# Memory tokens and first weights from one DMA queue, and query norms by four transposes, in a projection kernel with side work

## The chip, the cores and the metric

The kernel runs on one core of a Trainium2 chip. The metric is device time in microseconds (us) of one execution; lower is better. A core has a matrix engine (TensorE, PE in the profile, with its weight loads apart as PEld), VectorE (DVE), ScalarE (ACT), GpSimd (POOL), and SyncE (SP), which here only issues transfers. ACT issues a few transfers too. PSUM has eight banks of 128 x 512 f32, into which PE writes.

## The reference

One layer of a hybrid decoder over 256 tokens of width 2048. A combined input projection feeds a gated DeltaNet (12 query/key heads, 24 value heads of 128) and a four-head cross-attention into 256 memory tokens; both results are multiplied by a SiLU gate and go through an output projection. Cut to what the change touches:

```python
mem_n = rms_norm(mem, mem_norm_g)                       # 256 memory tokens
kv = jnp.einsum("bmd,de->bme", mem_n, w_kv)             # V and K of the memory
...
q = jnp.repeat(l2_norm(q), rep, axis=2) * DN_HEAD_DIM ** -0.5
k = jnp.repeat(l2_norm(k), rep, axis=2)
...
o = gated_delta_rule(q, k, v, g, beta)
o = rms_norm(o, out_g)
```

`l2_norm` of a query divides by the root of its sum of squares. The kernel leaves q unnormalised and puts that sum, `eq`, into the epsilon of the output's RMS norm, where it has the same effect.

## The kernel before

**Projections.** All big products are streams of weight tiles. `PLAN` lists 273 weight loads of 128 x 1024 f32 (512 KB): first the memory's V and K (`V0`, `V1`, `K0`, `K1`), then `ab`, and x, k, z, v, q column tiles, at the end the output projection (`o0` to `o3`). `wraw` issues a load into a tile `st` (five buffers); `wnext` splits it into a rounded half `hi` (ACT, a CAST, L342) and the rest `lo` (DVE, a subtraction, L346), both in one tile `wt` (four buffers). A projection in the form `proj_b` multiplies each tile by three products per half (activation hi by weight hi, hi by lo, lo by hi) and two row blocks, twelve matmuls of 128 x 512 into two banks (`pb`); `proj_a` does eight pairs of a 512- and a 256-wide matmul into one bank (`pa`).

**Start.** V0 and V1 go in turn over the same memory tokens. `memT` arrives as eight tiles `mst` of two 128-row steps each; `mem_prep` scales a step by a gain out of `prm` and splits it (`mkt`). The first step's `mkt` is made by a DVE TENSOR_SCALAR and a DVE SCALAR_TENSOR_TENSOR; the others' first half by ACT. `mem_prep` also squares the tokens (`msq`); `mem_stats` adds the squares, sums them over partitions on PE (`pss`), raises them to the power -1/2 on POOL (`msm`), and then `vm_done` scales V out of its bank (`vmh` on ACT, `vml` on DVE), which frees the bank. V0 and K0 use the two banks of pool `A`, V1 and K1 those of pool `pa`. Nine matmuls on zeros (`warm`) run on PE ahead of all.

**Order of the side work.** What is not a projection (convolutions, decays, triangular inverses `pm`, the delta rule, norms) is written as Python generators. While the program is written out, a clock `now` estimates PE's time; a generator that wants PE yields `("pe", gather)` and is entered into the stream when its `gather` time has passed, with all others that wait at that moment (`step_side`). `GATHER` (delta rule) is 0.5 us, `GATHER_Y` (the transposes `pyT` of finished outputs, generator `split_y`) 4.0 us. So these numbers set where in PE's program order such work stands; the engines run their queues in order. Up to `PINNED` = 45 us the order is kept as written.

**Delta rule.** `delta(g)` handles two pairs of heads, six groups in all: `pkq`, `pU`, `pO`, and at its end the second chunk's `pO` with the query norms. The query norms before: ACT squares q of each pair (tile `q2`, shown as `q`, read from `kq`), PE multiplies the squares by a column of ones (`pqs`, four one-column matmuls, f32, two records each) into a bank of pool `m`, and DVE reads four columns out of it (`eq`). Pool `m` has two banks and also serves `pkq`, `pyT`, `pm` and others.

**Names in the profile.** Nearly all operations go through two helpers, so their line is L86 (PE and SP) or L103 (ACT, DVE, POOL); the tile names tell them apart.

Of the kernel before, what the change touches and what calls it, by code (L numbers as in the profile page):

```python
# [21 lines left out]
NB = 2  # L22
C = 128
# [9 lines left out]

LOOK = 2
WARM = 9
GATHER = 0.5
GATHER_Y = 4.0
XPACE = 3.0
HOP = 0.25
PINNED = 45.0  # L40
# [32 lines left out]
def hybrid_kernel(ctx: ExitStack, tc: tile.TileContext, x, xT, memT, W, prm_d, cst_d, out):  # L73
# [3 lines left out]
    def pin(ins):  # L77

        return tc.keep_in_program_order(ins) if PINNED is None or now[0] < PINNED else ins
# [65 lines left out]
    def S2(name, shape, dt=F32):  # L145
        return s2p.tile([128] + list(shape), dt, name=name, tag="s2")
# [17 lines left out]
    def PS(tag, name):  # L164
        idle[tag].remove(min(idle[tag]))
        pt = ps.tile([128, 512], F32, name=name, tag=tag, bufs=PB[tag])
        held[id(pt)] = (tag, pt)
        return pt
# [4 lines left out]
    def give(pt, t):  # L173

        idle[held.pop(id(pt))[0]].append(t)
# [54 lines left out]
    def until(cond):  # L230
        while not cond():
            yield POLL
# [45 lines left out]
    def wraw():  # L278
# [20 lines left out]
        dma[0] = max(dma[0], free.pop(0)) + 1.46  # L299
        if n < 2:  # L300

            w = [slice(a * 512, (a + 1) * 512) for a in range(2)]
            if n == 0:
                pin(nc.scalar.dma_start(dst[:, w[0]], data[:, w[0]]))
                pin(nc.scalar.dma_start(prm[:, 0:P_CW], prm_d[:, 0:P_CW]))
            else:
                sy.dma_start(dst[:, w[0]], data[:, w[0]])
            sy.dma_start(dst[:, w[1]], data[:, w[1]])
            first_loads(1) if n == 0 else mem_load(2)
        else:  # L310
            sy.dma_start(dst, data)
            if 2 * n < NKT:
                mem_load(2 * n)
        wpos[0] += 1
        raws.append((n, kind, st, src, dma[0] + 2.0))

    def first_loads(a):

        if a == 0:
            mst[0] = S2("mst", [512])  # L320
        w = slice(a * 256, (a + 1) * 256)
        sy.dma_start(mst[0][:, w], memT[0][:, w])

    def wnext():
        while wpos[0] < len(PLAN) and free:
# [119 lines left out]
    def mem_load(k0):  # L445

        mst[k0 // 2] = S2("mst", [512])
        dma[0] += 0.75
        sy.dma_start(mst[k0 // 2], memT[k0 // 4][:, k0 % 4 * 256 : k0 % 4 * 256 + 512])
# [13 lines left out]
            se.activation(msq[-1], mst[k2], AF.Square)  # L463


    memq = [(2,), (3, 4), (5,), (6, 7), (8,), (9, 10), (11,), (12, 13), (14,), (15,)]

    def mem_piece(s):
        if not ahead:
# [773 lines left out]
    def delta(g):  # L1243
# [77 lines left out]
        for w in range(4):  # L1321
            se.activation(oq[:, w, :], B[:, w * C : (w + 1) * C], AF.Copy, scale=egc[:, 4 * g + w : 4 * g + w + 1])
        give(B, se.end)
        q2 = S2("q2", [2, 256])
        for i, p in enumerate(pp):
            se.activation(q2[:, i, :], KQ[p][:, 1, :], AF.Square)
        yield from pe_soon(GATHER)
        yield from until(lambda: spare("B") and spare("m"))
        B, pq = PS("B", "pO"), PS("m", "pqs")
        for w, i, h in heads:  # L1330
            mm(B[:, w * C : (w + 1) * C], aT[i][:, 1, h, :], u1[:, w, :], start=True, stop=True)
        for b in range(NB):
            for i in range(2):
                mm(pq[:, 2 * b + i : 2 * b + i + 1], q2[:, i, b * C : (b + 1) * C], ones, start=True, stop=True)
        yield 0.2
        ve.tensor_tensor(out=o[1], in0=B.rearrange("c (h e) -> c h e", h=4), in1=oq, op=ALU.add)
        give(B, ve.end)

        eq, e4 = SM("eq", [4], 2), SM("e4", [3, NB, 4], 2)
        ve.tensor_scalar(out=eq, in0=pq[:, 0:4], scalar1=EPS, scalar2=EPS * 128, op0=ALU.add, op1=ALU.mult)  # L1340
        give(pq, ve.end)
        ready.add(f"d{g}")
        yield
        for b in range(NB):
            for w in range(4):
                junk = SM("ojunk", [C])
                se.activation(junk, o[b][:, w, :], AF.Square, accum_out=e4[:, 0, b, w : w + 1])
        yield
        yield from until(lambda: {f"z{g}0", f"z{g}1"} <= ready)
        ev = [e4[:, a].rearrange("c b (i h) -> c (b i) h", h=2) for a in range(2)]  # L1350
        ve.scalar_tensor_tensor(out=ev[1], in0=ev[0], scalar=1.0 / 128,
# [54 lines left out]
            return proj_b(kts, x_act, "A" if t in (0, 6) else "pa", z_done(t))  # L1406
        return proj_a({"k": k_tile_done, "q": q_done}[kind](t))

    first_loads(0)
    spawn(mem_stats(), 8.0)  # L1410
    spawn(tok_prep(), 8.0)
    spawn(blank(), 100.0)
# [95 lines left out]
```

## Time and profile before

| | |
|---|---|
| median of three runs | 856.51 us (855.76 to 857.1) |
| the profiled execution, its own time | 857.04 us |
| its span in the trace | 855.3 us |
| granted clock of TensorE, mean over the span | 1.00 of full speed |
| PE busy | 848.0 us, 99% |
| weight loads of PE busy | 709.7 us, 83% |
| DVE busy | 618.1 us, 72% |
| ACT busy | 538.1 us, 63% |
| POOL busy | 46.5 us, 5% |

The span runs from the first to the last instruction; 1.74 us of the execution lie around it. The profiled execution is 0.53 us above the median of the runs. Busy shares are means over stages; which engine sets the time in a stage is read from the waits and from the chain of work that ended last.

### The profile page before, as it was taken

Reading aid. Unit: us, or ns where it says so; the run is one execution under the profiler, and the core shown is the slowest. Engines: PE = TensorE matmul, PEld = TensorE weight load, DVE = VectorE, ACT = ScalarE, POOL = GpSimd, SP = SyncE. Lnnn points to the kernel's source line nnn. Section 1 sums busy time; section 2 is a strip of 40 time slices with the busy share of each in tenths; the row PEclk is TensorE's granted clock in tenths of the full one; section 3 lists DMA queues with packets and bytes.
Section 4 is the critical chain, followed back from the end, with each engine's and each line's share of the span. In section 5 each row is a group of like instructions: output and inputs, shape, how many; then the busy total and the mean of one; then the engine's idle time right before and its main releaser. Section 6 shows DMA issues by size and latency. Waiting matters only on the chain.

```text
span 855.3 us, 13175 instructions
## 1 busy us (share of the span) xinstructions
PE 848.0 (99%) x4790; PEld 709.7 (83%) x4790; DVE 618.1 (72%) x1080; ACT 538.1 (63%) x929; POOL 46.5 (5%) x45
## 2 busy tenths in 40 slices
PE   9999999999999999999999999999999999999998
PEld 6888888888888888888888888788888888888886
DVE  6878886657779974788889989568886655454442
ACT  7656665798644765995966676679775654333331
POOL 1000000000000000001100202000010000000000
PEclk9999999999999999999999999999999999999999
DMA  9965566448677886869877769686755547666650
GB/s 344 335 218 177 171 189 165 146 147 263 197 208 241 263 243 180 261 210 266 226 243 218 227 214 279 198 242 222 227 158 169 186 142 265 214 210 205 199 197 25
DMA packets 145433, 181.59 MB, mean 212 GB/s; under 512 B 24824, under 2 KB 115824, under 8 KB 145368
## 3 DMA queue, kind: packets, MB, share of 16 engines
q1 hardware_dynamic: 145080, 180.47, 67.0%
q8 instruction: 37, 0.61, 0.3%
q10 hardware_dynamic: 288, 0.28, 0.1%
q14 instruction: 28, 0.23, 0.1%
HBM read 167.58 MB, written 6.89 MB: 204 GB/s over the span
## 4 chain that ended last, share of the span: by engine, by line
PE 95%; ACT 2%; DMA 1%; DVE 1%; issue 1%; SPq 0%; DVEq 0%
PE pb L86 72%; PE pa L86 13%; PE pO L86 2%; PE pU L86 2%; PE pm L86 1%; PE pkq L86 1%; PE pyT L86 1%; ACT dec L103 1%; DVE wt L346 1%; PE pqs L86 1%; PE pkk L86 1%; DMA erow<-dgc 0%; DMA st<-W_d 0%; ACT L103 0%; PE pab L86 0%
## 5 line engine op out<-in xcount | busy, mean ns | idle before, releaser
L346 DVE TENSOR_TENSOR wt<-st,wt 128x1024 fp32r<-128x1024 f32 (+1 forms) x275 | 331.9, 1212 | 164.9 <-ACT wt L342 161.2
L342 ACT CAST wt<-st 128x1024 fp32r<-128x1024 f32 (+1 forms) x275 | 286.3, 1045 | 224.3 <-PE pb L86 180.6
L86 PE MATMUL pb<-wt,hkt 128*128 128x512 f32 x1536 | 361.8, 392 | 0.0
L86 PEld LDWEIGHTS pb<-wt,hkt 128*128 128x128 f32 x1536 | 284.7, 188 | 58.7 <-DVE wt L346 0.4
L86 PE MATMUL pb<-wt,yhi 128*128 128x512 f32 x512 | 158.0, 390 | 0.0
L86 PE MATMUL pa<-hkt,wt 128*128 128x512 f32 (+1 forms) x768 | 142.8, 342 | 0.4 <-DVE wt L346 0.3
L86 PEld LDWEIGHTS pa<-hkt,wt 128*128 128x128 f32 x768 | 117.9, 188 | 18.3 <-DVE wt L346 1.0
L86 PEld LDWEIGHTS pb<-wt,yhi 128*128 128x128 f32 x512 | 95.7, 188 | 19.6
L86 PE MATMUL pb<-wt,ylo 128*128 128x512 f32 x256 | 99.7, 389 | 0.0
L86 PE MATMUL pb<-wt,mkt 128*128 128x512 f32 x384 | 88.6, 391 | 0.9 <-ACT wt L342 0.9
L86 PEld LDWEIGHTS pb<-wt,mkt 128*128 128x128 f32 x384 | 71.6, 188 | 16.8 <-ACT wt L342 1.8
L86 PEld LDWEIGHTS pb<-wt,ylo 128*128 128x128 f32 x256 | 48.1, 188 | 10.1
L103 ACT ACT_TABLE_LOAD x31 | 39.8, 1283 | 1.4 <-DVE acc L103 1.0
L103 DVE SCALAR_TENSOR_TENSOR acc<-raw,prm,acc 128x255 f32<-128x255 f32 (+2 forms) x72 | 34.2, 476 | 3.6 <-ACT acc L103 3.2
L103 DVE TENSOR_TENSOR inT<-inXT,inN 96x1 f32<-96x1 f32 (+22 forms) x92 | 29.1, 342 | 3.2 <-DMA inN<-dN 2.4
L103 DVE TENSOR_REDUCE inXT<-inT 96x1 f32<-96x1 f32 (+22 forms) x92 | 28.6, 337 | 0.7
L103 POOL TENSOR_TENSOR e<-e,mhalf 128x8 f32<-128x8 f32 x6 | 20.8, 3472 | 120.5 <-DVE e L103 120.5
L103 DVE TENSOR_TENSOR vc<-vc 128x512 f32<-128x512 f32 x36 | 24.5, 682 | 0.1
L103 POOL TENSOR_TENSOR srk<-skt,mhalf 128x4 f32<-128x4 f32 x6 | 7.0, 1175 | 224.6 <-DVE skt L103 145.6
L103 DVE SCALAR_TENSOR_TENSOR o<-o,e,zs 128x128 f32<-128x128 f32 x48 | 14.0, 345 | 7.0 <-POOL e L103 7.0
L103 ACT ACTIVATE ojunk<-o 128x128 f32<-128x128 f32 x48 | 14.4, 301 | 7.0 <-DVE o L103 4.9
L103 DVE TENSOR_TENSOR vc<-vc,vw 128x512 f32<-128x512 f32 x24 | 16.4, 683 | 2.8 <-DMA vc<-vs 2.8
(202 smaller groups left out, 693.9 us busy)
## 6 DMA issues: line engine op xcount, KB each, us to landing
st<-W_d SPq DMA_DIRECT2D x271, 512.0 KB
erow<-dgc SPq DMA_DIRECT2D x24, 256.0 KB
vw<-dtap SPq DMA_DIRECT2D x24, 256.0 KB
dN<-dec SPq DMA_DIRECT2D x12, 256.0 KB
n<-dN SPq DMA_DIRECT2D x12, 256.0 KB
vc<-vs SPq DMA_DIRECT2D x12, 224.0 KB
vc<-vc SPq DMA_DIRECT2D x12, 224.0 KB
xraw<-xT_d SPq DMA_DIRECT2D x8, 256.0 KB
```

The lines of the kernel that those rows point to most:

```text
L86: return lambda *a, **k: pin(getattr(self.eng, op)(*a, **k))
L103: return pin(getattr(self.eng, op)(*a, **k))
L342: pin(se.eng.copy(hi[:, w] if parts > 1 else hi, st[:, w] if parts > 1 else src))
L346: pin(ve.eng.tensor_tensor(out=lo[:, w] if parts > 1 else lo, in0=st[:, w] if parts > 1 else src, in1=hi[:, w] if parts > 1 else hi, op=AL ...
```

## The change

It has three parts. **Start:** ACT's queue issues only the gains `prm`; SP issues the first weight halves and the memory tokens in one row, and from there one memory tile after every second weight load. The memory steps are prepared one per load where they were sometimes two and sometimes one. **Gathering:** `GATHER` becomes 0.0 and `GATHER_Y` 0.5. **Query norms:** four PE transposes (`pqT`) put q of the four query blocks into a bank of pool `m`; ACT squares the bank into `q2` (128 x 512), which frees it; DVE sums each 128 columns (TENSOR_REDUCE) and applies the epsilon.

```diff
-GATHER = 0.5
-GATHER_Y = 4.0
+GATHER = 0.0
+GATHER_Y = 0.5
...
         if n < 2:
 
-            w = [slice(a * 512, (a + 1) * 512) for a in range(2)]
             if n == 0:
-                pin(nc.scalar.dma_start(dst[:, w[0]], data[:, w[0]]))
+                mst[0] = S2("mst", [512])
                 pin(nc.scalar.dma_start(prm[:, 0:P_CW], prm_d[:, 0:P_CW]))
-            else:
-                sy.dma_start(dst[:, w[0]], data[:, w[0]])
-            sy.dma_start(dst[:, w[1]], data[:, w[1]])
-            first_loads(1) if n == 0 else mem_load(2)
+            for a in range(2):
+                w, t = slice(a * 512, (a + 1) * 512), slice(a * 256, (a + 1) * 256)
+                sy.dma_start(dst[:, w], data[:, w])
+                if n == 0:
+                    sy.dma_start(mst[0][:, t], memT[0][:, t])
         else:
             sy.dma_start(dst, data)
-            if 2 * n < NKT:
-                mem_load(2 * n)
+
+        if n % 2 and n < 12 or n == 12:
+            mem_load(n + 1 if n % 2 else 14)
...
-    memq = [(2,), (3, 4), (5,), (6, 7), (8,), (9, 10), (11,), (12, 13), (14,), (15,)]
+    memq = [(k,) for k in range(2, 12)] + [(12, 13), (14,), (15,)]
...
-        q2 = S2("q2", [2, 256])
-        for i, p in enumerate(pp):
-            se.activation(q2[:, i, :], KQ[p][:, 1, :], AF.Square)
         yield from pe_soon(GATHER)
         yield from until(lambda: spare("B") and spare("m"))
-        B, pq = PS("B", "pO"), PS("m", "pqs")
+        B, pq = PS("B", "pO"), PS("m", "pqT")
         for w, i, h in heads:
             mm(B[:, w * C : (w + 1) * C], aT[i][:, 1, h, :], u1[:, w, :], start=True, stop=True)
-        for b in range(NB):
-            for i in range(2):
-                mm(pq[:, 2 * b + i : 2 * b + i + 1], q2[:, i, b * C : (b + 1) * C], ones, start=True, stop=True)
+        for w in range(4):
+
+            tr(pq[:, w * C : (w + 1) * C], KQ[pp[w % 2]][:, 1, w // 2 * C : (w // 2 + 1) * C])
...
-        ve.tensor_scalar(out=eq, in0=pq[:, 0:4], scalar1=EPS, scalar2=EPS * 128, op0=ALU.add, op1=ALU.mult)
-        give(pq, ve.end)
+        q2 = S2("q2", [4, C])
+        se.activation(q2.rearrange("c w e -> c (w e)"), pq, AF.Square)
+        give(pq, se.end)
...
+        ve.tensor_reduce(out=eq, in_=q2, axis=AX.X, op=ALU.add)
+        ve.tensor_scalar(out=eq, in0=eq, scalar1=EPS, scalar2=EPS * 128, op0=ALU.add, op1=ALU.mult)
```

The order of instructions moves at three places that matter below. The first is the start of SP's queue. The transfers into `st` are weights, those into `mst` memory tokens; 128x512 is half a weight tile. Before:

```order
L86 DMA mst<-memT_d 128x256
L86 DMA st<-W_d 128x512
L86 DMA mst<-memT_d 128x256
L86 DMA st<-W_d 128x512 x2
L86 DMA mst<-memT_d 128x512
L86 DMA st<-W_d 128x1024
L86 DMA mst<-memT_d 128x512
L86 DMA st<-W_d 128x1024
L86 DMA mst<-memT_d 128x512
```

The same place of the change:

```order
L86 DMA st<-W_d 128x512
L86 DMA mst<-memT_d 128x256
L86 DMA st<-W_d 128x512
L86 DMA mst<-memT_d 128x256
L86 DMA st<-W_d 128x512 x2
L86 DMA mst<-memT_d 128x512
L86 DMA st<-W_d 128x1024 x2
L86 DMA mst<-memT_d 128x512
L86 DMA st<-W_d 128x1024 x2
```

The first weight half, before issued by ACT ahead of `prm`, now stands at the head of SP's queue; up to the third weight tile (the first of 128x1024) the same transfers stand ahead, and behind it one memory tile follows two weight tiles.

The second place is PE's program at the end of V0, whose banks are `pb_116` and `pb_169` before, `pb_114` and `pb_163` in the change; V1's are the other two, and the first of K0 is the bank that comes last. Before:

```order
L86 MATMUL pss<-cst,msq 128x1 x2
L86 MATMUL pb_182<-wt,mkt 128x512 x3
L86 MATMUL pb_206<-wt,mkt 128x512 x3
L86 MATMUL pb_182<-wt,mkt 128x512 x3
L86 MATMUL pb_206<-wt,mkt 128x512 x3
L86 MATMUL pb_116<-wt,mkt 128x512 x3
L86 MATMUL pb_169<-wt,mkt 128x512 x3
L86 MATMUL pb_116<-wt,mkt 128x512 x3
L86 MATMUL pb_169<-wt,mkt 128x512 x3
L86 MATMUL pb_116<-wt,mkt 128x512 x6
L86 MATMUL pb_169<-wt,mkt 128x512 x6
```

The change:

```order
L86 MATMUL pb_114<-wt,mkt 128x512 x6
L86 MATMUL pb_163<-wt,mkt 128x512 x6
L86 MATMUL pss<-cst,msq 128x1 x2
L86 MATMUL pb_176<-wt,mkt 128x512 x3
L86 MATMUL pb_197<-wt,mkt 128x512 x3
L86 MATMUL pb_176<-wt,mkt 128x512 x3
L86 MATMUL pb_197<-wt,mkt 128x512 x3
L86 MATMUL pb_176<-wt,mkt 128x512 x6
L86 MATMUL pb_197<-wt,mkt 128x512 x6
L86 MATMUL pb_561<-wt,mkt 128x512 x6
```

The sum of the memory's squares (`pss`) stood ahead of V1's last but two and V0's last two loads and now stands behind them, 36 matmuls later: behind 168 of V's 192, where it stood behind 132.

The third place is the end of a group of the delta rule, on PE and on ACT. PE at the end of the second group, before:

```order
L86 MATMUL pa<-hkt,wt 128x512
L86 MATMUL pa<-hkt,wt 128x256
L86 MATMUL pO<-u_4711,aT 128x128 x4
L86 MATMUL pqs<-cst,q_4718 128x1 x4
L86 MATMUL pa<-hkt,wt 128x512
```

The change:

```order
L86 MATMUL pa<-hkt,wt 128x512
L86 MATMUL pa<-hkt,wt 128x256
L86 MATMUL pO<-u_4650,aT 128x128 x4
L86 MATMUL pqT<-cst,kq 128x128 x4
L86 MATMUL pa<-hkt,wt 128x512
```

ACT at the end of the first group, the change:

```order
L336 CAST wt<-st 128x1024
L103 ACTIVATE q_4120<-pqT 128x512
L103 ACTIVATE ojunk,e_4119<-o 128x128 x4
L336 CAST wt<-st 128x1024
L103 COPY raw<-pa 128x512
L103 ACTIVATE dec<-erow,gcc 128x128 x2
L103 ACT_TABLE_LOAD
L103 ACTIVATE kq<-acc 128x256
L103 ACTIVATE dec<-erow,gcc 128x128 x2
L103 ACTIVATE acc<-raw,prm 128x256
L103 ACTIVATE vc<-vc 128x512 x2
L103 ACTIVATE vc<-vc,sV 128x128 x8
```

The transposes stand where the one-column matmuls stood (in the first group alone, ahead of `pO`). On ACT the square of the transposed queries stands behind a CAST; a little later a row of side work runs from `raw` to `vc` with no CAST in it.

## Rows read from the trace of the kernel before

**Rows 1.** The page, parts 1 and 4: busy time by engine; the chain by engine.

```profile
PE 848.0 (99%) x4790; PEld 709.7 (83%) x4790; DVE 618.1 (72%) x1080; ACT 538.1 (63%) x929; POOL 46.5 (5%) x45
...
PE 95%; ACT 2%; DMA 1%; DVE 1%; issue 1%; SPq 0%; DVEq 0%
```

**Rows 2.** Waits of PE: us in total, times, longest us.

```profile
PE pb L86 <- ACT wt L342: 0.9, 1, 0.9
PE pa L86 <- DVE wt L346: 0.3, 1, 0.3
```

**Rows 3.** Timeline, first 12 us: start, length, instruction, idle before and its releaser.

```profile
0.72 0.41 ACTq L304 DMA_DIRECT2D st<-W_d  x1
...
0.73 0.39 SPq L86 DMA_DIRECT2D mst<-memT_d  x1
...
1.16 0.46 ACTq L305 DMA_DIRECT2D prm<-prm_d  x1
...
1.21 4.02 PE L86 MATMUL warm<-warm 128*128 128x512 bf16 x9 [1.21 <-DVE warm L103]
...
4.61 1.36 ACT L342 CAST wt<-st 128x512 fp32r<-128x512 f32 x2 [1.67 <-DMA st<-W_d]
...
5.61 0.35 DVE L103 TENSOR_SCALAR mkt<-mst,prm 128x256 fp32r<-128x256 f32 x1 [4.46 <-DMA prm<-prm_d]
...
6.12 4.27 PE L86 MATMUL pb<-wt,mkt 128*128 128x512 f32 x17 [0.89 <-ACT wt L342]
...
8.91 1.05 ACT L342 CAST wt<-st 128x1024 fp32r<-128x1024 f32 x1 [0.73 <-DMA st<-W_d]
...
9.99 1.23 DVE L346 TENSOR_TENSOR wt<-st,wt 128x1024 fp32r<-128x1024 f32 x1 [0.30 <-ACT wt L342]
```

**Rows 4.** Busy time by engine from the first projection matmul to `pss`.

```profile
core 0: us, PE busy (x) PEld busy (x) DVE busy (x) ACT busy (x) POOL busy (x), PEclk, DMA share, GB/s
5.90:36.46 30.56, 30.34 (x135) 24.91 (x135) 28.27 (x44) 25.69 (x42) 0.00 (x0) 1.00 1.01 380
```

**Rows 5.** Chain of work that ended last, up to 40 us: start, length, what.

```profile
6.12 30.34 PE pb L86 x132
```

**Rows 6.** The chain at the end of the first group.

```profile
407.18 0.56 PE pqs L86 x6
407.75 3.31 PE pb L86 x14
```

**Rows 7.** The chain at the end of the second group.

```profile
459.97 1.53 PE pa L86 x9
...
462.39 0.79 PE pqs L86 x8
463.18 2.19 PE pa L86 x12
```

**Rows 8.** The chain around four transposes of the cross-attention's queries.

```profile
196.53 0.44 PE xpT L86 x4
196.97 3.23 PE pb L86 x14
```

**Rows 9.** Tile `pyT`: minimum/median/maximum ns of one, first and last start.

```profile
L86 PE MATMUL pyT<-cst,o x48: 270/272/273, 639.6 to 712.5; 128*128 128x128 f32 x48
```

**Rows 10.** Tiles `dg` and `q`: a DVE sum over 128x512, and ACT's squares.

```profile
L103 DVE TENSOR_REDUCE skt<-dg x6: 678/686/687, 189.9 to 393.9; 128x4 f32<-128x512 f32 x6
...
L103 ACT ACTIVATE q<-kq x12: 429/436/456, 405.7 to 685.1; 128x256 f32<-128x256 f32 x12
```

**Rows 11.** Timeline behind `pss`: the power, and V scaled out of its banks.

```profile
37.40 1.07 POOL L103 TENSOR_TENSOR msm<-msm,mhalf 128x2 f32<-128x2 f32 x1 [32.67 <-DVE msm L103]
...
43.85 0.69 ACT L103 ACTIVATE vmh<-pb,msm 128x512 fp32r<-128x512 f32 x1 [3.09 <-PE pb L86]
...
45.88 0.75 DVE L103 SCALAR_TENSOR_TENSOR vml<-pb,msm,vmh 128x512 fp32r<-128x512 f32 x1 [0.55 <-ACT vmh L103]
```

**Rows 12.** Busy time by engine in a stretch in which ACT ran no CAST.

```profile
418.30:423.30 5.00, 5.00 (x24) 4.14 (x23) 3.41 (x10) 4.97 (x13) 0.00 (x0) 1.00 1.08 355
```

More of the change, by code (lines that the diff above doesn't have):

```diff
@@ L300, in wraw @@
         if n < 2:
-            w = [slice(a * 512, (a + 1) * 512) for a in range(2)]
             if n == 0:
-                pin(nc.scalar.dma_start(dst[:, w[0]], data[:, w[0]]))
+                mst[0] = S2("mst", [512])
                 pin(nc.scalar.dma_start(prm[:, 0:P_CW], prm_d[:, 0:P_CW]))
-            else:
-                sy.dma_start(dst[:, w[0]], data[:, w[0]])
-            sy.dma_start(dst[:, w[1]], data[:, w[1]])
-            first_loads(1) if n == 0 else mem_load(2)
+            for a in range(2):
[3 more added lines that the diff above has]
+                    sy.dma_start(mst[0][:, t], memT[0][:, t])
         else:
             sy.dma_start(dst, data)
-            if 2 * n < NKT:
-                mem_load(2 * n)
+        if n % 2 and n < 12 or n == 12:
+            mem_load(n + 1 if n % 2 else 14)
         wpos[0] += 1
         raws.append((n, kind, st, src, dma[0] + 2.0))
[L317 to L322, printed above, removed]
     def wnext():
@@ L1407, in process @@
         return proj_a({"k": k_tile_done, "q": q_done}[kind](t))
-    first_loads(0)
     spawn(mem_stats(), 8.0)
```

## The prediction

> **What bounds the kernel now.** I read the page first: PE is busy 99% of the span, every other engine 83% or less, and the chain of work that ended last is 95% PE [rows 1]. So a microsecond counts only where PE's own stream gets shorter, or where PE waits. The waits of PE come next: besides the opening and bursts of tiny matmuls there are two, 0.9 us for the first split weight tile and 0.3 us for one later tile [rows 2]. Side work is therefore priced by what it puts into PE's stream, and ACT, DVE and DMA work at nothing as long as weight tiles arrive in time. The opening is the exception, so I read its timeline [rows 3]: the warm-up on zeros ends at 1.21 + 4.02 = 5.23 us, the first real matmul starts at 6.12, and from there 132 matmuls run in 30.34 us, 0.230 us each, with no gap [rows 5]. In that stretch DMA share is 1.01 at 380 GB/s [rows 4]: transfers land by the bytes ahead of them.
>
> **Query norms.** Removed from PE: eight one-column records per group, in the chain 0.79 us [rows 7]. They also cost the stream behind them something. After them twelve `pa` matmuls take 2.19 us, where nine before take 1.53, so twelve would take 2.04: a drag of 0.15. In the first group, where they were split, the second part takes 0.56 and the fourteen `pb` behind it 3.31 instead of 14 x 0.230 = 3.22, a drag of 0.09 [rows 6]. I take 0.92 per group (0.79 + 0.13). Added: four 128x128 f32 transposes. The same operation on cross-attention queries takes 0.44 for four, and the fourteen `pb` behind it 3.23, no drag [rows 8]. I take 0.45. The saving is 0.47 a group, 2.8 us over six. The bounds: 1.9 us if the drag stays with the transposes (0.79 - 0.44 = 0.35, rounded down for the split groups to 0.32), 2.8 if it goes; I take the upper one, because the row behind the transposes shows no drag.
>
> One record of a transpose lasts 0.270 to 0.273 us [rows 9], but four end 0.44 us after the work ahead of them [rows 8], 0.11 each: they overlap. The Trainium skill says otherwise (page "TensorE: Matmul & The Clock Gate", Part 4, PE-mode transpose): about 275 ns for a 128x128 transpose in a kernel. By that price four are 1.10 us and the norms would lose about 1.1 us over six groups. The chain here does not agree with it as a step, only with the length of a record.
>
> On ACT two squares of 0.436 us go [rows 10] and one of 128x512 out of PSUM comes, near in size to `vmh`, 0.69 [rows 11]: 0.2 us less a group. On DVE a sum over 128x512 comes, 0.686 us on `dg` [rows 10], 4.1 us over six groups. It stands behind the outputs' squares on a queue that is 72% busy [rows 1]; what covers it is the lead of the split weight tiles, which let PE wait for DVE 0.3 us in the whole run [rows 2]. Without that cover it costs up to 4.1 us. The bank of pool `m` comes free with ACT's square instead of a short DVE read; that is a rival below.
>
> **Start.** The first matmul waits for two things: the first split half (its CAST is the first of two in 1.36 us from 4.61, so done near 5.29) and the scaled tokens. The page names ACT, but the DVE multiply ran from 5.61 to 5.96, after 4.46 us of waiting for `prm`, which ACT's queue issued second, at 1.16, behind half a weight tile [rows 3]. So the gains were late. In the change they are issued first, at 0.72, with nothing ahead on their queue; the tokens go behind one half weight on SP, but these are the bytes that also landed before (the CAST starts at 4.61), so I expect tokens and gains by 4.7 and the multiply done by 5.2. Then the CAST and the warm-up bound: first matmul near 5.35, a gain of 0.77. What is late next is the third weight tile. Up to it the same bytes are ahead, so its CAST stays at 8.91 and its DVE rest ends at 9.99 + 1.23 = 11.22. PE wants that rest with the 26th matmul, 6.12 + 25 x 0.230 = 11.87; 0.65 us of margin, so a start 0.77 earlier waits 0.1 there. Behind it one memory tile fewer is ahead of the fourth weight tile (256 KB at 380 GB/s, 0.7 us), so that one comes earlier too. I take 0.65. Bounds: 0, if tokens land as late as `prm` did; 0.89, the whole wait that the timeline shows.
>
> The Trainium skill (page "DMA: Bandwidth & Descriptors", Issuing engines are not separate DMA queues) says that several issuers save only the time to issue. The issues here take 0.39 to 0.46 us each [rows 3]; by this rule alone, the half weight issued at 0.73 instead of 0.72 loses nothing and the tokens one issue, 0.4 us, which the end of the warm-up hides.
>
> The sum of the memory's squares moves 36 matmuls back, to 5.35 + 168 x 0.230 = 44 us. Behind it wait POOL's power (1.07), and V's two scalings (0.69 and 0.75 each bank) [rows 11]; PE wants the first of these banks for K0 at 5.35 + 192 x 0.230 + 0.4 = 49.9 (0.4 for `pss` itself, half of the eight records of [rows 7]). Unhindered the first bank is free at 44.4 + 1.07 + 0.69 + 0.75 = 46.9; with one CAST (1.05) and one DVE rest (1.23) ahead [rows 3] at 49.2. Hidden, with 0.7 to 3 us to spare; I take 0. Without the cover it would cost what it is late, once.
>
> **Gathering.** Delta pieces enter PE's stream alone instead of with company. A break in the stream would show as a drag behind it; behind four transposes it is 0.01 us [rows 8], behind the one-column work 0.09 to 0.15, which I have counted. Nothing for the rest. Finished outputs reach their transposes earlier, but PE in the output projection waits for nothing [rows 2], so that gains nothing either.
>
> **Sum.** The profiled execution is 857.04 us; its span 855.3 and 1.74 around it. 857.04 - 2.8 - 0.65 = 853.6. That execution is 0.53 above the median of the runs, so I predict 853.1 for the median of 856.51, 0.4% faster.
>
> **Rivals.** A change within 0.2%, 1.7 us, can't be told from none here; faster means below 854.8, slower above 858.2.
> - *Forecast*, 853.1: both terms. Chance 0.62.
> - *Only the norms pay.* PE waits at the third weight tile or the tokens are late: 853.8. For it: 0.65 us of margin only. Against: the same bytes are ahead. 0.13.
> - *Start in full and waits shrink.* The start gives 0.89, and the 0.9 + 0.3 us of waits [rows 2] fall away in part because side work is spread: 851.9. Nothing in particular speaks for it. 0.06.
> - *ACT's clump.* In the first group ACT now runs `raw` to `vc` without a CAST. A like stretch of 5 us before kept ACT busy 4.97 of 5.00 with PE never idle [rows 12]. The new one has a `raw`, an `acc` and four small `dec` more; by the nearest rows that is 0.69 for the one (512 columns out of PSUM, as `vmh` [rows 11]) and at most 0.44 for each other (`q` [rows 10]), 2.9 us in all. If none of it is covered by the split tiles that lie ahead, PE waits that long once: 856.0; half of it gives 854.6. 0.12.
> - *Transposes at their record's length.* Four times 0.272 [rows 9] is 1.09 instead of 0.45: the norms lose 6 x 0.17 = 1.0, the start gives 0.65, so 856.9, no change. That is the page's price named above; the chain speaks against it. 0.03.
> - *The bank held by ACT*, the slower side. Each group's square stands behind a CAST and other ACT work, and the next user of pool `m` waits on PE with all projections queued behind it. ACT is seen busy 4.97 us without pause [rows 12]; if the square stands behind most of that, PE waits up to some 3 us a group. From 0.85 us a group (5.1 us in six: the 3.4 gained and 1.7 beyond) the kernel is slower; at 1.2 us it stands at 860.3. Against: pool `m` has two banks, and the square alone is 0.7. 0.04.
>
> Faster 0.81 (the first three), same 0.15, slower 0.04. The range: 851.6 to 855.2 holds the forecast, the norms alone, the best case and part of the clump, about 0.8.
>
> **What would show it.** The first `pb` starts near 5.35 us, and the multiply ends before the first CAST does; if it starts after 5.8, the start's step is wrong. The chain shows four `pqT` at about 0.44 us, and the stretch behind them without drag; at 0.8 or more the norms' step is wrong. PE's busy time falls by about 3 us. K0 starts without a wait near 49.9 us. A new row in PE's waits, on ACT's CAST near 400 us or on the query square, would make the prediction wrong.

## Result and profile after

The change made the kernel slower: 859.99 us median of 13 runs (858.77 to 864.78) against 857.23 of 13 runs of the kernel before (855.76 to 860.24), ratio 1.0035 with a 95% interval of 1.0025 to 1.0045. The forecast was 853.1, in a range of 851.6 to 855.2. Two executions lie far outside and enter no ratio, one of the kernel before (2193.76 us) and one of norms_shift_prm below (1052.25). The profiled execution has a span of 858.8 us against 855.3 and a mean granted clock of 0.998 against 1.000.

The page of the changed kernel, parts 1 and 4 [rows 1]:

```profile
PE 848.3 (99%) x4766; PEld 708.0 (82%) x4766; DVE 622.4 (72%) x1086; ACT 538.0 (63%) x923; POOL 44.4 (5%) x45
...
PE 80%; DVE 6%; DMA 4%; issue 3%; ACT 3%; POOL 2%; SPq 1%; DVEq 0%; POOLq 0%; ACTq 0%
```

PE has 24 matmuls fewer (four in each of six groups), but as many busy microseconds, where the forecast had about 3 us less; 1.7 us of them are matmuls at half clock (last section). The chain is PE for 80% where it was 95%; the rest goes through DVE, DMA, ACT and POOL. The waits of PE say for what [rows 2]: us in total, times, longest.

```profile
PE pb L86 <- DVE wt L340: 2.6, 3, 1.5
PE pm L86 <- ACT Y L103: 1.3, 1, 1.3
...
PE pU L86 <- DVE ul L103: 0.6, 1, 0.6
PE pa L86 <- DVE wt L340: 0.3, 1, 0.3
PE pm L86 <- issue: 0.2, 1, 0.2
```

Waits for split weight tiles went from 1.2 us to 2.9, and two waits for side results (`Y`, `ul`) are new.

**The norms on PE cost what was forecast.** The chain at the end of the first group (start, length, what) and tile `pqT`'s own records:

```profile
397.96 0.44 PE pqT L86 x4
398.40 1.76 PE pa L86 x10
```

```profile
L86 PE MATMUL pqT<-cst,kq x24: 271/272/273, 397.8 to 693.2; 128*128 128x128 f32 x24
L103 ACT ACTIVATE q<-pqT x6: 587/596/599, 408.5 to 693.5; 128x512 f32<-128x512 f32 x6
```

Four transposes end 0.44 us after the work ahead of them though one record lasts 0.272, and the ten `pa` behind them take 0.176 each, near the 0.170 of an undisturbed row [rows 7]. So the 275 ns that the Trainium skill gives ("TensorE: Matmul & The Clock Gate", Part 4, PE-mode transpose) is the length of a record here, and not what a transpose adds to PE's stream.

**The start comes earlier and then waits.** The timeline of the first 13 us [rows 3]:

```profile
0.72 0.41 ACTq L304 DMA_DIRECT2D prm<-prm_d  x1
...
0.73 0.39 SPq L86 DMA_DIRECT2D st<-W_d  x1
...
4.18 0.69 DVE L103 TENSOR_SCALAR mkt<-mst,prm 128x256 fp32r<-128x256 f32 x1 [3.03 <-DMA mst<-memT_d]
...
5.02 6.89 PE L86 MATMUL pb<-wt,mkt 128*128 128x512 f32 x25
...
10.31 1.05 ACT L336 CAST wt<-st 128x1024 fp32r<-128x1024 f32 x1 [0.87 <-DMA st<-W_d]
...
11.39 1.23 DVE L340 TENSOR_TENSOR wt<-st,wt 128x1024 fp32r<-128x1024 f32 x1 [1.43 <-ACT wt L336]
...
12.67 1.66 PE L86 MATMUL pb<-wt,mkt 128*128 128x512 f32 x6 [0.76 <-DVE wt L340]
```

The gains no longer hold the multiply: it runs 1.4 us earlier (4.18 for 5.61), and the first matmul starts at 5.02, the end of the warm-up, 1.1 us earlier. But the third weight tile's CAST starts at 10.31, where it started at 8.91, and PE waits for it, at last 0.76 us for its rest from DVE, until 12.67. The chain shows what that comes to, before and in the change:

```profile
36.45 0.34 PE pss L86 x4
```

```profile
45.40 0.34 PE pss L86 x4
```

The second is behind 168 matmuls and ends at 45.74. Before, `pss` stood behind 132 and ended at 36.45 + 0.34 = 36.79; 36 more at 0.230 make 45.07. The start loses 0.7 us in this pair of profiles.

**The middle.** Busy time in three stretches; columns as in [rows 4]. The kernel before, then the change:

```profile
400.00:430.00 30.00, 30.00 (x142) 24.49 (x141) 25.87 (x46) 28.14 (x64) 3.80 (x5) 1.00 0.84 239
...
480.00:530.00 50.00, 50.00 (x261) 42.37 (x260) 46.59 (x94) 31.92 (x66) 0.52 (x1) 1.00 0.79 247
545.00:560.00 15.00, 13.95 (x365) 11.01 (x359) 3.68 (x3) 12.39 (x25) 0.51 (x1) 1.00 0.59 216
```

```profile
400.00:430.00 30.00, 28.15 (x133) 22.69 (x132) 28.16 (x57) 25.99 (x58) 5.28 (x5) 1.00 0.81 239
...
480.00:530.00 50.00, 49.18 (x250) 40.62 (x249) 45.00 (x88) 31.05 (x61) 0.51 (x1) 1.00 0.76 232
545.00:560.00 15.00, 13.36 (x335) 10.85 (x323) 7.54 (x15) 12.31 (x25) 1.03 (x2) 0.92 0.70 239
```

PE is idle 1.9 us more in the first stretch, 0.8 more in the second, and 0.6 more in the third, where the clock is also lower. In these stretches the side engines are nearly as full as PE: before, ACT 94% in the first and DVE 93% in the second, where the means over the span are 63% and 72%. The longest wait of PE, 1.5 us, ends at 423.49. It is read from the timelines of PE, DVE and ACT:

```profile
423.49 3.94 PE L86 MATMUL pb<-wt,hkt 128*128 128x512 f32 x16 [1.52 <-DVE wt L340]
```

```profile
415.36 1.21 DVE L340 TENSOR_TENSOR wt<-st,wt 128x1024 fp32r<-128x1024 f32 x1
418.11 1.14 DVE L103 SCALAR_TENSOR_TENSOR o<-o,e,zs 128x128 f32<-128x128 f32 x4 [1.54 <-POOL e L103]
...
422.21 2.36 DVE L340 TENSOR_TENSOR wt<-st,wt 128x1024 fp32r<-128x1024 f32 x2
```

```profile
411.36 1.05 ACT L336 CAST wt<-st 128x1024 fp32r<-128x1024 f32 x1 [1.06 <-DMA st<-W_d]
...
417.15 2.44 ACT L103 ACTIVATE vc<-vc,sV 128x128 f32<-128x128 f32 x8
419.49 1.98 ACT L336 CAST wt<-st 128x1024 fp32r<-128x1024 f32 x2
```

ACT runs from 412.4 to 419.5 without a CAST; that is the row of side work from `raw` to `vc` that the prediction named. The CAST is done near 420.5, but on DVE the rest of that tile stands behind the scalings of the outputs `o`, which waited 1.5 us for POOL's power, and other side work, and starts at 422.21. Two rows of side work, one on each engine, fall on one weight tile. The chain goes through POOL's power and DVE, and not through ACT:

```profile
413.98 4.11 POOL e L103
418.11 1.14 DVE o L103 x4
```

With DVE free at 420.5, the rest (1.2 us) would have been done near 421.7, before PE came to this tile near 422.0: an estimate from these rows. So ACT's row alone would have cost next to nothing here.

### The profile page after: what moved, and what is told of

It is laid out like the page before. It is cut to its first block, busy times and chain, and to the rows that moved or that the text cites. A ratio compares the mean times of both kernels' runs of the same rounds, so it can differ in the third digit from the quotient of the medians.

```text
span 858.8 us, 13129 instructions
## 1 busy us (share of the span) xinstructions
PE 848.3 (99%) x4766; PEld 708.0 (82%) x4766; DVE 622.4 (72%) x1086; ACT 538.0 (63%) x923; POOL 44.4 (5%) x45
## 4 chain that ended last, share of the span: by engine, by line
PE 80%; DVE 6%; DMA 4%; issue 3%; ACT 3%; POOL 2%; SPq 1%; DVEq 0%; POOLq 0%; ACTq 0%
PE pb L86 61%; PE pa L86 10%; DVE wt L340 2%; DMA st<-W_d 2%; POOL e L103 2%; PE pU L86 1%; PE pO L86 1%; PE pm L86 1%; DVE vc L103 1%; PE pkq L86 1%; ACT wt L336 1%; PE pyT L86 1%; DMA vc<-vs 1%; DVE acc L103 1%; ACT dec L103 1%
## 5 line engine op out<-in xcount | busy, mean ns | idle before, releaser
L86 PE MATMUL pb<-wt,hkt 128*128 128x512 f32 x1536 | 362.1, 392 | 2.0 <-DVE wt L340 1.9
L86 PEld LDWEIGHTS pb<-wt,hkt 128*128 128x128 f32 x1536 | 284.5, 188 | 62.4 <-DVE wt L340 3.6
L86 PE MATMUL pb<-wt,yhi 128*128 128x512 f32 x512 | 158.2, 390 | 0.0
L86 PE MATMUL pa<-hkt,wt 128*128 128x512 f32 (+1 forms) x768 | 142.5, 341 | 0.4 <-DVE wt L340 0.3
L86 PEld LDWEIGHTS pa<-hkt,wt 128*128 128x128 f32 x768 | 118.1, 188 | 18.3 <-DVE wt L340 1.0
L86 PEld LDWEIGHTS pb<-wt,yhi 128*128 128x128 f32 x512 | 95.7, 188 | 19.7
L86 PE MATMUL pb<-wt,ylo 128*128 128x512 f32 x256 | 99.6, 389 | 0.0
L86 PE MATMUL pb<-wt,mkt 128*128 128x512 f32 x384 | 89.7, 393 | 0.8 <-DVE wt L340 0.8
L86 PEld LDWEIGHTS pb<-wt,mkt 128*128 128x128 f32 x384 | 71.2, 188 | 18.0 <-DVE wt L340 1.9
L86 PEld LDWEIGHTS pb<-wt,ylo 128*128 128x128 f32 x256 | 48.1, 188 | 9.9
L103 ACT ACTIVATE dec<-erow,gcc 128x128 f32<-128x128 f32 x48 | 16.5, 395 | 6.7 <-DMA erow<-dgc 6.5
L103 ACT COPY raw<-pa 128x512 f32<-128x512 f32 x24 | 13.9, 583 | 6.4 <-PE pa L86 6.0
```

The source lines that it names most:

```text
L86: return lambda *a, **k: pin(getattr(self.eng, op)(*a, **k))
L103: return pin(getattr(self.eng, op)(*a, **k))
```

## Experiments

Each is timed against runs of the kernel before on the same chip; the ratio and its interval are to that kernel.

**start_only.** The kernel before with the first hunk of the diff (start, pace, `memq`) alone.

> Only the start of the change (transfers, pace of the memory tokens, one memory step per load). Theory A, the start loses: the first matmul comes near 5.0 us, but the third weight tile lands after 10 us and PE waits for it, so the sum of the memory's squares ends 0.6 to 0.8 us later than before and the time is 0.5 to 0.9 us above the kernel before. Rival, the slow landing was chance of one profiled execution: the third tile lands near 8.9 us and the time is 0.5 to 0.8 us below.

Measured 857.78, ratio 1.0007 (0.9997 to 1.0017). First matmul at 5.02, the third tile's CAST at 10.46, `pss` at 45.52: the landing is no chance of one execution. In the profile the loss is 0.8 us (45.52 + 0.34 = 45.86 for 45.07); in the runs it is not told from nothing. A likely reason, not shown, is in the kernel before: in some of its executions the clock rises late and costs more than the wait costs here (last section).

**norms_only.** The hunks of `delta` alone, `GATHER` 0.5 and 4.0.

> Only the query norms by transposes, gathering as before. Theory B, the norms save on PE and the loss in the middle comes from the gathering (another order of side work, in which ACT runs 7 us without a CAST): 2 to 2.8 us below the kernel before. Rival C, the norms themselves bring the loss (a sum on DVE and a square on ACT ahead of the splitting of weight tiles): no change, or above.

Measured 865.98, ratio 1.0099 (1.0081 to 1.0116): theory B falls; it loses far more than the whole change. In its profile the longest wait of PE names no releaser (`PE pb L86 <- issue: 3.0, 1, 3.0`, up to 588.60), and from 589.7 on follow 10.2 us at half clock; both are taken up below.

**gather_only.** Only this:

```diff
-GATHER = 0.5
-GATHER_Y = 4.0
+GATHER = 0.0
+GATHER_Y = 0.5
```

> Only the gathering times 0.0 and 0.5, query norms and start as before. Theory B: 2 to 5 us above the kernel before, with waits of PE for split weight tiles between 405 and 425 us and near 550 us. Rival C: within 0.5 us of it.

Measured 861.28, ratio 1.0046 (1.0027 to 1.0065). As theory B has it, but rival C's half came true as well: each part alone loses. The 12 runs fall into two groups: 858.25 to 859.49 at a mean granted clock of 0.999 or 1.000, and 863.07 to 866.24 at 0.996 to 0.998. So the order costs 1 to 2 us here, and 6 to 9 in the executions in which the clock falls.

**norms_gather.** Both, start as before.

> Query norms and gathering of the change, start as before. If the parts add: what the change loses without its start, 2 to 2.5 us above the kernel before (theory A with the start at 0.7), with the same waits near 420, 510 and 554 us as the change. If the start only shifted where the waits fall: about 1 us or more away from that.

Measured 858.94, ratio 1.0024 (1.0011 to 1.0036): together they lose less than either alone (8.7 and 4.0 us by the medians). With the start's 0.0007 that makes 1.0031, inside the change's interval. The parts do not add; what they share is the order of the side work.

**prm_first.** Only ACT's two transfers exchanged.

```diff
-                pin(nc.scalar.dma_start(dst[:, w[0]], data[:, w[0]]))
                 pin(nc.scalar.dma_start(prm[:, 0:P_CW], prm_d[:, 0:P_CW]))
+                pin(nc.scalar.dma_start(dst[:, w[0]], data[:, w[0]]))
```

> The kernel before with only ACT's two first transfers exchanged, gains ahead of the half weight tile. Theory (gains were late, and the loss at the start comes from putting all weights and tokens on one queue): the multiply starts near 4.5 us, the first matmul comes between 5.2 and 5.6, the third weight tile lands at 8.8 to 9.8 as before, and the time falls by 0.3 to 0.8 us. Rival (whatever lets PE start earlier makes it wait at the third tile for the same length): first matmul earlier, but the sum of the memory's squares ends at the same 36.8 us and the time is unchanged.

Measured 857.33, ratio 0.9997 (0.9986 to 1.0008). The first matmul still starts at 6.13, since now the half tile lands later (its CAST starts at 5.46 for 4.61); neither theory's path, and no gain. What an earlier first matmul is worth with the transfers of the kernel before can be read from the profile of gather_only, whose start is the same; in that execution the gains came 0.8 us earlier:

```profile
5.30 6.75 PE L86 MATMUL pb<-wt,mkt 128*128 128x512 f32 x25
...
12.21 2.11 PE L86 MATMUL pb<-wt,mkt 128*128 128x512 f32 x8 [0.16 <-DVE wt L346]
```

PE starts at 5.30 for 6.12 and then waits for the third weight tile, whose CAST starts at 9.86 for 8.91; `pss` ends at 37.19, 0.4 us later than in the kernel before.

**one_queue.** The first half tile on SP's queue, gains alone on ACT's, the old pace of tokens.

```diff
-                pin(nc.scalar.dma_start(dst[:, w[0]], data[:, w[0]]))
                 pin(nc.scalar.dma_start(prm[:, 0:P_CW], prm_d[:, 0:P_CW]))
-            else:
-                sy.dma_start(dst[:, w[0]], data[:, w[0]])
+            sy.dma_start(dst[:, w[0]], data[:, w[0]])
+            if n == 0:
+                first_loads(0)
             sy.dma_start(dst[:, w[1]], data[:, w[1]])
```

> The kernel before with gains alone on ACT's queue and the first weight half on SP's, memory tokens at the old pace (one after each weight tile). If the one queue makes the landings slow: the third weight tile lands after 10 us as in the change, and PE waits there. If the new pace (a fourth weight tile close behind the third) makes them slow: it lands near 8.9 us and the first 132 projection matmuls end 0.5 us or more earlier than before.

Measured 857.9, ratio 1.0012 (1.0003 to 1.0022). The third tile's CAST starts at 10.18: the pace is not it. In the six traces with all weights and tokens on one queue it starts at 10.12 to 10.91; in the fourteen with the half tile on ACT's queue at 8.77 to 9.86. Busy time and rate of the transfers from 4 to 6 and from 6 to 8.5 us, before and in this kernel (the last two columns are DMA share and GB/s):

```profile
4.00:6.00 2.00, 1.23 (x3) 0.15 (x1) 0.35 (x1) 1.26 (x3) 0.73 (x1) 1.00 1.07 392
6.00:8.50 2.50, 2.38 (x10) 1.74 (x11) 2.50 (x5) 2.07 (x4) 0.00 (x0) 1.00 1.04 394
```

```profile
4.00:6.00 2.00, 2.00 (x5) 0.98 (x4) 1.84 (x3) 0.61 (x2) 0.73 (x1) 1.00 0.76 200
6.00:8.50 2.50, 2.50 (x11) 2.02 (x10) 1.45 (x4) 1.61 (x4) 0.00 (x0) 1.00 1.00 333
```

From 4 to 6 us the queues are less busy (0.76 for 1.07), and in both stretches a given busy share moves fewer bytes: 0.38 MB less in the first and 0.15 in the second. Why stays open.

**plus_onecol.** The change with the removed PE work put back ahead of the transposes.

```diff
+        for w in range(4):
+            te.matmul(pq[:, w : w + 1], KQ[pp[w % 2]][:, 1, w // 2 * C : (w // 2 + 1) * C], ones, start=True, stop=True)
         for w in range(4):
 
             tr(pq[:, w * C : (w + 1) * C], KQ[pp[w % 2]][:, 1, w // 2 * C : (w // 2 + 1) * C])
```

> The change with four one-column matmuls put back on PE ahead of the four transposes in each group (results overwritten by the transposes; nothing else moves: the order on PE, ACT and DVE stays that of the change but for one swap in the output projection). This is the price of what was removed. By the step of the prediction (0.92 us a group where PE bounds): 5.5 us above the change. If PE waits anyway behind these places and swallows the work: 0 to 3 us above. If the one-column matmuls cost nothing in the stream: unchanged.

Measured 860.59, ratio 1.0040 (1.0028 to 1.0052): 0.6 us above the change's 859.99, and the two intervals overlap. The profiles, both of 858.8 us, show where most of the rest of the 5.5 us went: PE's idle time falls from 10.5 to 8.1 us, and the stretch at half clock, which cost the change's profiled execution 1.7 us, is gone (mean granted clock 1.000 for 0.998). In the order of the change PE's stream alone is not what sets the time.

**before_double.** The same work added to the kernel before, whose order on ACT and DVE it leaves as it is.

```diff
+                te.matmul(pq[:, 2 * b + i : 2 * b + i + 1], q2[:, i, b * C : (b + 1) * C], ones, start=True, stop=True)
                 mm(pq[:, 2 * b + i : 2 * b + i + 1], q2[:, i, b * C : (b + 1) * C], ones, start=True, stop=True)
```

> The kernel before with the one-column matmuls done twice, without the scheduler's clock, order on ACT and DVE unchanged. By the prediction's step 5.5 us above the kernel before, since PE waits almost nowhere there. If the side engines set the pace even in the kernel before, 0 to 3 us above.

Measured 862.24, ratio 1.0060 (1.0048 to 1.0073), 5.1 us (4.1 to 6.3): the forecast's price of 0.92 us a group, 5.5 us, holds there.

**no_norm_pe.** The work taken out of the kernel before, the scheduler's clock advanced by its estimate.

```diff
-        for b in range(NB):
-            for i in range(2):
-                mm(pq[:, 2 * b + i : 2 * b + i + 1], q2[:, i, b * C : (b + 1) * C], ones, start=True, stop=True)
+        now[0] += 4 * 0.19
```

> The kernel before without the one-column matmuls (left out: the sum over the query's elements; four of the squares stand for it), the scheduler's clock advanced as if they were there, so that the order of the rest hardly changes. By the prediction's step (PE bounds, 0.92 us a group) 5.5 us below the kernel before. Theory (between 350 and 560 us DVE and ACT are nearly as full as PE, so that PE time saved there turns into waits): less than half of it, 0 to 2.5 us below.

Measured 854.44, ratio 0.9965 (0.9951 to 0.9978), 3.0 us of 5.5. Between the two theories. Where the rest went is in the chain near 550 us (below).

**no_sum.** The change without DVE's TENSOR_REDUCE.

```diff
-        ve.tensor_reduce(out=eq, in_=q2, axis=AX.X, op=ALU.add)
-        ve.tensor_scalar(out=eq, in0=eq, scalar1=EPS, scalar2=EPS * 128, op0=ALU.add, op1=ALU.mult)
+        ve.tensor_scalar(out=eq, in0=q2[:, :, 0], scalar1=EPS, scalar2=EPS * 128, op0=ALU.add, op1=ALU.mult)
```

> The change without DVE's sum over the query squares (left out: the sum; the first square of each query stands for it). If the 4.1 us that the sum adds to a nearly full DVE are what is lost in the middle: 2 to 4 us below the change. If the order of the side work is what loses: within 1.5 us of the change, up or down with the order.

Measured 859.49, ratio 1.0029 (1.0019 to 1.0039), 0.5 us below the change, which is not told from nothing. But the scheduler's clock moved as well, and the order on PE differs from the change's in hundreds of instructions, so this run alone does not show the price of the sum. That the 4.1 us on DVE are not what is lost rests on norms_same, which has them.

**norms_held.** norms_only with one line behind the transposes, so that the scheduler's clock runs as with the old work.

```diff
             tr(pq[:, w * C : (w + 1) * C], KQ[pp[w % 2]][:, 1, w // 2 * C : (w // 2 + 1) * C])
+        now[0] += 4 * (0.19 - 0.093)
```

> Query norms by transposes alone, gathering and start as before, the scheduler's clock advanced by the price of the one-column matmuls instead of the transposes. The same on the chip as the run with the norms alone but for the order. Theory (the order decides, not the operations): several us away from the 8.5 us that the norms alone lost, between 2 us below and 4 us above the kernel before. Rival (the operations themselves lose): 6 to 10 us above again.

Measured 862.95, ratio 1.0068 (1.0055 to 1.0080). Not in the theory's range, and below the rival's. Some 3 us come from one line that adds no instruction; the order on PE still differs from that of the kernel before nearly as much as in norms_only.

**norms_same.** The transposes in the place of the old matmuls, square and sum in the place of the old read, and every estimate of the scheduler as before.

```diff
-        for i, p in enumerate(pp):
-            se.activation(q2[:, i, :], KQ[p][:, 1, :], AF.Square)
+        se.run(2 * 0.274)
...
+        for w in range(4):
+            te.transpose(pq[:, w * C : (w + 1) * C], KQ[pp[w % 2]][:, 1, w // 2 * C : (w // 2 + 1) * C], ident)
+            now[0] += 0.19
...
+        nc.scalar.activation(q2.rearrange("c a b -> c (a b)"), pq, AF.Square)
+        nc.vector.tensor_reduce(out=eq, in_=q2.rearrange("c a (b e) -> c (a b) e", b=2), axis=AX.X, op=ALU.add)
```

> The kernel before with the query norms by transposes, square and sum where the read of the bank stood, and the scheduler's clock and estimates advanced as before, so that the order of all other work stays nearly that of the kernel before (37 rows of PE's order differ, where the norms alone moved over 400). If the order is what loses, the 2.8 us that the prediction gave to the norms come out, less what is swallowed: 1 to 2.8 us below the kernel before. If the operations lose (a longer hold of the bank, sum on DVE): above it by 2 us or more, as the two other runs with the norms alone.

Measured 856.95, ratio 0.9992 (0.9981 to 1.0003). The same operations that lost 8.7 us in one order and 5.7 in another lose nothing in this one. So the order is what lost. But the gain of 2.8 us does not come out either.

**norms_same2.** As that, the sum behind the squares of the outputs.

> As the run before it, but DVE's sum stands behind the squares of the outputs, where the change has it. If its place matters little: within 1 us of that run. If a sum standing just ahead of the power on POOL delays the outputs' scaling: 1 us or more above it.

Measured 857.86, ratio 1.0003 (0.9995 to 1.0012), 0.9 us above norms_same, within the 1 us of the expectation: its place matters little.

**after_lead** and **before_lead.** One split weight tile more.

```diff
-LOOK = 2
+LOOK = 3
...
-    s2p = ctx.enter_context(tc.tile_pool(name="s2p", bufs=62))
+    s2p = ctx.enter_context(tc.tile_pool(name="s2p", bufs=58))
...
-    wp = ctx.enter_context(tc.tile_pool(name="wp", bufs=4))
+    wp = ctx.enter_context(tc.tile_pool(name="wp", bufs=5))
```

> The change with one weight tile more of lead (five split tiles for four, loads three ahead for two; four fewer of the 62 general tiles). Theory (the middle loses because split tiles arrive late behind rows of ACT and DVE side work): the waits of PE for split tiles near 420 and 490 to 515 us go, and the time falls by 2 to 4 us below the change, to 856 to 858. Rival (PE waits for side results and loses clock, not for weight tiles): within 1 us of the change.

> Control for the longer lead: the kernel before with five split weight tiles, loads three ahead and four general tiles fewer. If the lead itself takes the loss (general tiles short, another order): 5 us or more above the kernel before, as the change with it was above the change. If it hurts only the change's order: within 2 us of the kernel before.

Measured 868.53 (ratio 1.0137, 1.0120 to 1.0155) and 864.94 (1.0084, 1.0071 to 1.0097). Both lose 7.5 us or more against their own base, so the lead itself, or the order it brings, loses, and the first run says nothing on the change. Inconclusive.

**before_shift, norms_shift, norms_shift_prm.** The traces above have one more wait in common. In the chain near 550 us PE stands without a releaser ("issue") in a burst of tiny matmuls `pm` of the inverse. The chain of norms_same, then of no_norm_pe:

```profile
548.33 0.68 PE pm L86 x46
549.01 1.70 issue
550.71 1.72 PE pm L86 x83
```

```profile
547.69 0.82 PE pm L86 x57
548.51 2.45 issue
550.97 1.02 PE pm L86 x64
```

The kernel before has the same wait, from 549.38 to 550.21:

```profile
549.38 0.83 issue
```

PE came 0.4 and 0.9 us earlier in the two others and went on 0.5 and 0.8 us later: what was gained ahead of this place is lost in it. Busy time from 0 to the middle of the stop, with the counts of PE's matmuls and weight loads, before and in no_norm_pe:

```profile
0.00:549.80 549.80, 546.87 (x3152) 457.53 (x3152) 440.31 (x846) 374.29 (x657) 38.01 (x39) 1.00 0.72 225
```

```profile
0.00:550.00 550.00, 546.10 (x3152) 456.39 (x3153) 440.31 (x846) 374.38 (x657) 38.43 (x39) 1.00 0.72 225
```

The stop comes behind the same number of instructions though different work stands there. These three kernels shift the program by tiny matmuls ahead of everything (57 in the two with the norms of norms_same, 49 in the first); the third has prm_first's exchange as well.

```diff
-WARM = 9
+WARM = 7
...
+    for _ in range(57):
+        te.matmul(wps[0:32, 0:32], warm[0:32, 0:32], warm[0:32, 0:32], start=True, stop=True)
```

> The kernel before with 49 tiny matmuls (32x32) in place of two of the nine warm-up matmuls: 94 instructions more on PE ahead of everything, nothing else moved. In all kernels so far PE stopped near 550 us at the same place of its own instruction count, in the middle of a burst of tiny matmuls of the inverse, where the profile sees no releaser. If that is the arrival of the next piece of PE's program, the place now falls ahead of the burst and the 0.8 us wait there goes; the time falls by 0 to 1 us. Rival (the wait belongs to the data of the inverse): it stays at 0.8 us in the same place of the burst.

> Query norms by transposes in the order of the kernel before, with 110 instructions more on PE ahead of everything (57 tiny matmuls for two of the warm-up). That order lost 1.7 us to a wait in the burst near 550 us and ran 3.4 us at half clock behind it. If the wait is the program's arrival: both go, and the time falls to 853.5 to 855 us, 2.5 to 3.5 us below the kernel before. If the wait is the data's: 856 to 857.5, as without the shift.

> As the run before it, with the gains first on ACT's queue. If the early multiply helps once PE can run on: 0.3 to 0.8 us below that run. As measured for the gains alone: the same.

Measured 858.96 (1.0014, 1.0003 to 1.0026), 857.36 (1.0007, 0.9994 to 1.0020) and 859.91 (1.0026, 1.0015 to 1.0036). Chain and counts of norms_shift:

```profile
548.96 1.45 PE pm L86 x107
550.41 2.02 issue
552.43 0.38 PE pm L86 x18
```

```profile
0.00:551.50 551.50, 547.99 (x3279) 458.10 (x3279) 442.26 (x849) 373.88 (x654) 38.05 (x39) 1.00 0.73 224
```

The stop has moved within the burst and stands behind 3279 and 3279 instructions, 254 more than in the other kernels (before_shift: 3280 and 3280, 256 more). So it belongs to a place in PE's program, not to the inverse's data. Other kernels bear this out: before_double has its only wait of PE without a releaser (0.7 us) behind 3280 and 3280, and norms_only and norms_held, with 3.0 and 1.7 us, behind 3408 and 3408 and behind 3407 and 3408, twice 256 more than the kernel before. The trace also shows transfers of 16 KB on an instruction queue, 37 in the kernel before; at 256 instructions each that is 9472 of the 9580 that PE has recorded. In the eleven traces in which the moment was read, PE goes on 2.2 to 2.6 us after such a transfer begins (in the kernel before it begins between 547.7 and 547.8 us and takes 0.9). That half of the expectation holds; what sets the moment at which a transfer begins stays open. The other half fails: the next such place, 256 instructions on, falls into the same burst, and the wait stays (1.3 us in before_shift, 2.0 here). No version that keeps the sum of the squares beats the kernel before by more than the measurement can tell. The third has the shortest span of all profiled executions, 853.1 us, and yet a ratio of 1.0026; what sets its runs apart was not tried.

## Why the prediction was wrong

- **What bounds the kernel.** The step that failed is the first: "a microsecond counts only where PE's own stream gets shorter, or where PE waits", and with it side work "priced by what it puts into PE's stream". It holds in the order of the kernel before where PE's stream gets longer (before_double: 5.1 us for 5.5 of work), half where it gets shorter (no_norm_pe: 3.0 of 5.5), and not in the order of the change (plus_onecol: 0.6 us for the same work). I read the other engines' load as a mean over the span, 72% and 63% [rows 1]; in the stretches of the delta rule DVE and ACT are at 93 and 94%, and in the wait read above a weight tile is late where two rows of side work fall together.
- **Gathering** was given "nothing". It is the term whose price was most wrong: alone it costs 4.0 us by the median, 1 to 2 in the runs without a fall of the clock. I priced breaks in PE's stream (which cost next to nothing, 0.06 us behind the first transposes) and not what the new order does on ACT and DVE, nor the clock behind the waits that it makes.
- **Query norms.** The size of the PE term was right: 0.44 us for four transposes, and 5.1 us for the old work twice. The operations themselves lose nothing (norms_same). The gain of 2.8 us is swallowed in every order that was run: by waits for side work and the clock behind them in the change, and in norms_same, as far as its profile shows, by the stop at 549 us, 0.9 us longer than before, and by 3.4 us at half clock behind it, which cost 1.7.
- **ACT's clump**, a rival at 0.12, came at its place, but the wait there (1.5 us) was for DVE's rest of the tile, behind POOL's power, which I did not name. That is also the new row in PE's waits: on DVE, and not on ACT's CAST.
- **Start.** The gains were late, as said, and the first matmul comes at 5.02, earlier than the 5.35 forecast. Wrong was what followed from "the same bytes are ahead". They are, but they do not land as early: on one queue the CAST of the third weight tile starts at 10.31 and not at 8.91, so the half weight at the head of SP's queue was not free. Nor would the 0.65 us have come with the old landing for certain: in gather_only's profile the first matmul is 0.8 us earlier and `pss` 0.4 later. The rival "only the norms pay" should have been "the start loses". In the runs that comes to 0.0007, which is no difference.
- **The wait of PE for its program** stood in the waits of the kernel before as a row that names no releaser (`PE pm L86 <- issue: 1.0, 2, 0.8`), which [rows 2] does not show; I left it aside with the bursts of tiny matmuls. In the six kernels counted in which it stands at the same place as before, PE goes on at 550.2 to 551.7 us, and what was saved ahead is lost there.
- **DVE's sum and the bank held by ACT**: with the sum in the old order nothing is lost (norms_same); no wait of PE for the bank stands in the waits. `pss` and K0 ran without a wait, as forecast.

Shown are the order as the cause of the loss, PE's two prices, the one queue as the cause of the late tile, and the program's place as that of the stop. Only read from the traces, and not tried alone, is which single move of the order makes each wait, and how the loss is shared between the waits and the lower clock behind them.

## What to carry to other kernels

Where a scheduler interleaves side work, price a change by stretches, and look there at the engine that prepares the next tile: at 93% of DVE, an edit that only changes numbers in the order can cost more than the work it saves. Before trusting a saving on the bounding engine, double the work in the old order and in the new; if it costs little in the second, something else sets the time. To test an operation apart from its schedule, hold the scheduler's estimates at their old values.

## What the runs showed of the hardware

- **PE's program arrives in pieces.** In or just behind a burst of tiny matmuls PE stopped for 0.2 to 3.0 us behind 6302 to 6305 recorded instructions in six kernels, behind 6558 to 6560 in four and behind 6815 or 6816 in two: steps of 256, each ending 2.2 to 2.6 us after a 16 KB transfer on the instruction queue began, where that was read.
- **The clock falls behind a stretch with waits.** In the change, PE was busy 2.26 of 3.60 us, and the granted clock was 0.50 for the 3.4 us after it:

```profile
554.00:557.60 3.60, 2.26 (x29) 1.34 (x29) 0.00 (x0) 3.51 (x7) 0.00 (x0) 1.00 0.50 151
557.60:561.00 3.40, 3.40 (x73) 3.40 (x69) 1.23 (x1) 2.94 (x8) 0.51 (x1) 0.50 0.13 36
```

  At 0.50 (1.2 GHz) four matmuls of 128x512 take 1.73 us in norms_same (552.43 to 554.16), 0.43 each for 0.23 [rows 5]. norms_only had 10.2 us of it, worth 5.1, behind a wait of 3.0. The change's own runs part by it: six of 858.77 to 859.86 us at a mean granted clock of 0.999 or 1.000, seven of 859.99 to 864.78 at 0.998 or less.
- **The first rise of the clock varies.** In the profile of the kernel before the first matmuls of the projection already take 0.23 us; in before_double, with the same start, nine are counted from 6.1 to 10.0 us, 0.43 each, and `pss` starts 1.7 us later:

```profile
6.10:10.00 3.90, 3.90 (x9) 3.07 (x10) 3.63 (x8) 3.10 (x6) 0.00 (x0) 1.00 1.04 359
```

  The clock column (the third from the end) reads 1.00 here all the same, so this is read from the length of a matmul, which is that at half clock. In norms_gather, with that start as well, `pss` starts at 38.08 us for 36.45. The runs of the kernel before lie between 855.4 and 861.1 us over all comparisons, and in such a spread a start that is 1 us better or worse does not show.
